# Layout changes by DVE blocks and DMA in place of TensorE transposes, in a two-layer mLSTM + RG-LRU trunk

## The chip, the cores and the metric

The kernel runs on one core of a Trainium2 chip. The metric is the device time of one execution in microseconds; where several runs are given, their median. A profile is one more execution, recorded instruction by instruction. Engines: PE (TensorE: matmuls; PEld its weight loads), DVE (VectorE), ACT (ScalarE), POOL (GpSimd), SP (SyncE, which here only issues DMAs).

## The reference

Two layers of one mixer, then a final RMSNorm; batch 1, 256 positions, width 2048, all in float32. Cut to what matters:

```python
def hybrid_layer(x, ...):
    u = rms_norm(x, norm_g)
    qk, v, o, z_a, ig, fg, xb, z_b = split(u @ w_in)            # w_in 2048 x 12304
    q, k = split(silu(causal_dwconv(qk, qk_conv)))              # 8 heads, width 128; v: width 256
    h = mlstm_chunkwise(q, k * DK ** -0.5, v, ig + i_bias, log_sigmoid(fg + f_bias))
    h = layernorm_per_head(h * sigmoid(o)) * head_norm_g
    y_a = h * silu(z_a)
    xc = causal_dwconv(xb, lru_conv_w) + lru_conv_b
    y_b = rg_lru(xc, w_a, b_a, w_x, b_x, lam) * silu(z_b)       # h_t = a_t h_(t-1) + u_t
    return x + concatenate([y_a, y_b]) @ w_out                  # w_out 4096 x 2048
for l in range(2): x = hybrid_layer(x, ...)
return rms_norm(x, final_g)
```

## The kernel before

Weights pass once from DRAM through SBUF. Every float32 product is made of three matmuls with split operands: H (high part, rounded to the fast float32 form) times H, H times L (the rest), L times H. For activations the split parts are `x_s` (the layer's input, channels on partitions), `yaH`/`yaL` and `ybH`/`ybL` (outputs of the two branches); for weights `wH` (cast on ACT, L289) and `wL` (subtraction on DVE, L160).

The work of a layer is cut into four groups `g` of 512 columns (two heads, 512 recurrent channels). A group has the chunks `o`, `qk`, `v`, `xb`, `z`, `zb` (each x times 2048 x 512 of `w_in`), a `gate` unit (the recurrent gates' matrices) and, for the group before, four `out` chunks. A chunk is four units of 1 MB of weights; a unit is two halves, and a half is 12 matmuls of 128 x 128 by 512 columns. `_sequence` lists the units in the order in which PE takes them. The last loop of `tile_trunk` goes over the halves: it prepares the split of the half three further on (`AHEAD`), records the half's matmuls, calls its `after` function (evacuation of the accumulator) and then `pump`, which lets the generators in `bg` (conv, attention, gates, norms) record some of their steps up to a budget. `None` or `"wait"` from a generator ends its turn. `require(key)` runs generators until a result is recorded. The split buffers are four deep (`wsp`), the raw weights three units (`wraw`). Each engine then runs its instructions in the order in which they stand; only data decide when.

Accumulators of the usual form hold tokens on partitions. Where channels are wanted on partitions there are three ways. PE transposes 128 x 128 blocks with an identity (L651 `ps_ty` for `ya`, 8 for each layer and group, in `z_post`; L851 `ps_tx` for the next layer's input, 8 for each of 4 chunks, in `out_chunk`). `to_channels` (for `qk`, `xb` and `zb`) writes a permuted copy `tok`, transposes 32 x 32 blocks on DVE (L404, `blk`), writes the rows to DRAM by four DMAs of SP (L407, `moved`) and reads them back by one of POOL (L408, `fr`). And a chunk named by `_by_channel` (only `zb` of layer 0, group 3) is multiplied with the operands exchanged (`mm_b`, L321), so that channels come out on partitions at once.

At the layers' border the four last `out` chunks add to `x_acc`; each is squared and summed for the norm, stored, transposed and split into the next layer's `x_s` (`split_xT`, L807 and L163). Layer 1 starts with its chunk `o`; the gates' scan (`gates_gen`, tiles `scs`) and the small transposition of `sT` (L495) hang on the end of that chunk.

## Time and profile before

| | us |
|---|---|
| median of 3 runs | 1513.75 (1512.88 to 1514.87) |
| the profiled execution | 1514.09 |
| its span in the trace | 1512.4 |
| PE busy | 1494.3 (99%) |
| DVE busy | 1040.6 (69%) |
| ACT busy | 907.0 (60%) |

A page's groups give, for one line, engine, operation and tile: count, busy time, mean duration in ns, and the idle time of the engine just before with what ended it. A timeline row gives start, duration, engine, line, operation, tiles written and read, form and count; in brackets the idle time of the engine before it and its releaser. A windows row gives from:to, length, the busy time and count of PE, PEld, DVE, ACT and POOL, PE's granted clock, the DMA engines' busy share and GB/s. A row of the waits: who waited for whom, total, times, longest.

### The profile page before, as it was taken

How to read it: one execution, taken by the hardware profiler on the slowest of the kernel's cores; microseconds unless marked ns; L12 is line 12 of the kernel's file. 1: busy time of each engine (PE TensorE's matmuls, PEld its weight loads, DVE VectorE, ACT ScalarE, POOL GpSimd, SP SyncE). 2: the span in 40 equal slices, each digit the busy share in tenths (PEclk: the TensorE clock that was granted, in tenths of full speed). 3: DMA queues.
4: the chain of work that ended last, by engine and by line, in shares of the span. 5: the costliest groups of instructions: out<-in, count | busy, mean ns of one | idle time of the engine just before them, and what ended most of it. 6: DMA issues, size and time to landing. Idle time of an engine off the chain costs nothing.

```text
span 1512.4 us, 18554 instructions
## 1 busy us (share of the span) xinstructions
PE 1494.3 (99%) x6980; PEld 1248.3 (83%) x6980; DVE 1040.6 (69%) x1406; ACT 907.0 (60%) x1142; POOL 66.4 (4%) x127
## 2 busy tenths in 40 slices
PE   8999999999999999999999999999999999999997
PEld 6888888888888888888888888888888888888886
DVE  6778666876567754778657786567855678556775
ACT  6658545675456754558654685466755567555674
POOL 0001000100000000000000000001000000000002
PEclk9999999999999999999999999999999999999999
DMA  9764658756577566885665656678566775577773
GB/s 329 286 212 168 217 214 250 233 191 223 192 254 225 193 223 213 256 255 195 213 205 191 229 177 221 209 232 245 181 221 218 230 231 198 200 229 268 233 244 108
DMA packets 82729, 333.07 MB, mean 220 GB/s; under 512 B 9024, under 2 KB 23376, under 8 KB 61136
## 3 DMA queue, kind: packets, MB, share of 16 engines
q1 hardware_dynamic: 72128, 299.40, 57.0%
q0 software_dynamic: 7760, 27.81, 8.1%
q10 hardware_dynamic: 2752, 4.69, 0.9%
q8 instruction: 54, 0.88, 0.2%
q14 instruction: 35, 0.29, 0.1%
HBM read 300.91 MB, written 30.95 MB: 219 GB/s over the span
## 4 chain that ended last, share of the span: by engine, by line
PE 91%; DMA 4%; DVE 3%; ACT 1%; issue 1%; SPq 0%; ACTq 0%; DVEq 0%
PE acc L307 27%; PE acc L306 27%; PE acc L308 27%; DMA raw<-in_ws_dram 3%; PE ps_gt L699 3%; PE acc L321 1%; DVE wL L160 1%; DVE xc L163 1%; PE acc L927 0%; ACT wH L289 0%; PE acc L928 0%; PE acc L929 0%; PE ps_ty L651 0%; DMA nb<-nG_d 0%; DMA nG_d<-scs 0%
## 5 line engine op out<-in xcount | busy, mean ns | idle before, releaser
L160 DVE TENSOR_TENSOR wL<-raw,wH 128x1024 fp32r<-128x1024 f32 (+1 forms) x526 | 638.1, 1216 | 362.9 <-ACT wH L289 362.3
L289 ACT CAST wH<-raw 128x1024 fp32r<-128x1024 f32 (+1 forms) x526 | 549.0, 1047 | 426.2 <-PE acc L308 394.0
L306 PE MATMUL acc<-wH,x_s 128*128 128x512 f32 x1504 | 587.9, 391 | 6.3 <-ACT wH L289 6.3
L307 PE MATMUL acc<-wL,x_s 128*128 128x512 f32 x1504 | 587.4, 391 | 2.0 <-DVE wL L160 2.0
L308 PE MATMUL acc<-wH,x_s 128*128 128x512 f32 x1504 | 586.4, 390 | 0.0
L306 PEld LDWEIGHTS acc<-wH,x_s 128*128 128x128 f32 x1504 | 283.0, 188 | 64.8 <-ACT wH L289 6.5
L307 PEld LDWEIGHTS acc<-wL,x_s 128*128 128x128 f32 x1504 | 283.0, 188 | 62.7 <-DVE wL L160 4.9
L308 PEld LDWEIGHTS acc<-wH,x_s 128*128 128x128 f32 x1504 | 283.0, 188 | 58.6
L306 PE MATMUL acc<-wH,yaH 128*128 128x512 f32 x224 | 87.9, 392 | 0.0
L306 PE MATMUL acc<-wH,ybH 128*128 128x512 f32 x224 | 87.4, 390 | 0.0
L308 PE MATMUL acc<-wH,yaL 128*128 128x512 f32 x224 | 87.3, 390 | 0.0
L308 PE MATMUL acc<-wH,ybL 128*128 128x512 f32 x224 | 87.3, 390 | 0.0
L307 PE MATMUL acc<-wL,ybH 128*128 128x512 f32 x224 | 87.3, 390 | 0.0
L307 PE MATMUL acc<-wL,yaH 128*128 128x512 f32 x224 | 87.2, 389 | 0.0
L401 ACT ACTIVATE tok<-acc,rstd 128x512 f32<-128x512 f32 x46 | 29.1, 685 | 38.2 <-PE acc L308 38.2
L308 PEld LDWEIGHTS acc<-wH,yaL 128*128 128x128 f32 x224 | 42.0, 188 | 9.0
L308 PEld LDWEIGHTS acc<-wH,ybL 128*128 128x128 f32 x224 | 42.0, 188 | 8.9
L307 PEld LDWEIGHTS acc<-wL,ybH 128*128 128x128 f32 x224 | 42.1, 188 | 8.3
L306 PEld LDWEIGHTS acc<-wH,ybH 128*128 128x128 f32 x224 | 42.1, 188 | 8.3
L307 PEld LDWEIGHTS acc<-wL,yaH 128*128 128x128 f32 x224 | 42.1, 188 | 8.1
L306 PEld LDWEIGHTS acc<-wH,yaH 128*128 128x128 f32 x224 | 42.1, 188 | 8.1
L832 ACT COPY stage<-acc 128x1024 f32<-128x1024 f32 x24 | 24.4, 1015 | 38.9 <-PE acc L308 38.9
(209 smaller groups left out, 1332.8 us busy)
## 6 DMA issues: line engine op xcount, KB each, us to landing
raw<-in_ws_dram SPq DMA_DIRECT2D x168, 1024.0 KB, 4.9
raw<-in_ws_dram SPq DMA_DIRECT2D x190, 512.0 KB, 4.8
x_d<-stage POOLq DMA_DIRECT2D x24, 512.0 KB, 6.8
moved<-blk SPq DMA_DIRECT2D x92, 128.0 KB, 2.3
fr<-moved POOLq DMA_DIRECT2D x23, 512.0 KB, 4.8
x_d<-x_acc ACTq DMA_DIRECT2D x8, 512.0 KB, 8.0
x_acc<-x_d SPq DMA_DIRECT2D x8, 512.0 KB, 5.0
xp<-in_xt_dram SPq DMA_DIRECT2D x8, 256.0 KB, 7.9
```

Of the source, the lines that this page charges most:

```text
L160: return V.tensor_tensor(out=o, in0=a, in1=b, op=op)
L163: return V.scalar_tensor_tensor(out=o, in0=a, scalar=s, in1=b, op0=op0, op1=op1)
L289: S.copy(out=H[:, o], in_=r[:, o])
L306: PE.matmul(o, a_H[:, kt, tsl], Hv[:, k], start=s, stop=False)
L307: PE.matmul(o, a_H[:, kt, tsl], Lv[:, k], start=False, stop=False)
L308: PE.matmul(o, a_L[:, kt, tsl], Hv[:, k], start=False, stop=e)
L321: PE.matmul(ps[:, ct, T * part : 2 * T], W[:, k, P * ct : P * ct + P], moving, start=first and k == 0 and part == 0, stop=last and k == 3 ...
L401: S.activation(out=tok[:, :, :, t, :].rearrange("p m c j -> p c m j"), in_=acc[:, t, :].rearrange("p (c m j) -> p c m j", c=4, m=4), func= ...
L699: PE.matmul(o, W[:, ib, jl], xs[:, ib, a, :], start=j == 0 and i == 0 and W is Hv and a == 0, stop=i == 1 and W is Lv, skip_group_check=True)
L832: S.copy(out=stage, in_=ps)
```

## The change

Six things change.

1. PE transposes no more 128 x 128 blocks. `ya` goes the way of `to_channels`: `z_post` writes `tok` by DVE, `swapped` does the 32 x 32 transposition and the DMAs, `split_channels` makes `yaH` and `yaL` out of `fr`, after `LANDING` (4) turns. The next layer's input goes the same way in `out_chunk`, with a second pair of `tok`/`blk` in the buffer `qs` for the odd chunks.
2. The border's splits are no generator: they are recorded a fixed number of halves (`BORDER`, 7) after their chunk.
3. The first two chunks of layer 1, `o` and `qk`, go by turns unit by unit; each unit's quarter of the contraction needs one quarter of `x_s`. The last four `out` chunks: the first two still by turns, the others one after the other.
4. `zb` of group 0 comes before `z` of the same group (it came in group 1); group 1 has `qk`, `o`, `v`.
5. `zb` of group 3 goes by channel in layer 1 too.
6. `require` and `drain` go round the generators where one says "wait"; the transposition of `sT` waits two (layer 0) or four (layer 1) turns more; `zb` waits for `hz`, the product of head output and gate, instead of `yT`.

```diff
@@ _sequence
-            head = {0: ("o", "qk", "v"), 1: ("o", "zb", "v", "qk")}.get(g, ("o", "v", "qk"))
-            items = [("in", l, k, 0 if k == "zb" else g) for k in head]
+            head = {0: ("o", "qk", "v"), 1: ("qk", "o", "v")}.get(g, ("o", "v", "qk"))
+            items = [("in", l, k, g) for k in head]
             items += fill[0:2] + [("in", l, "xb", g)] + fill[2:4]
-            items += [("in", l, "z", g), ("gate", l, g)] + ([("in", l, "zb", g)] if g > 0 else [])
-            seq += [u for it in items for u in units(it)]
+            items += [("in", l, "z", g), ("gate", l, g)]
+            items.insert(len(items) if g > 0 else -2, ("in", l, "zb", g))
+            us = [u for it in items for u in units(it)]
+            if l > 0 and g == 0:
+                us[0:8] = [us[i] for i in (0, 4, 1, 5, 2, 6, 3, 7)]
+            seq += us
         if l + 1 < DEPTH:
-            for c in (0, 2):
-                u = units(("out", l, NG - 1, c)) + units(("out", l, NG - 1, c + 1))
-                seq += [u[i] for i in (0, 2, 1, 3)]
+            u = [u for c in range(4) for u in units(("out", l, NG - 1, c))]
+            seq += [u[i] for i in (0, 2, 1, 3, 4, 5, 6, 7)]
@@ _by_channel
-    return (l, kind, g) == (0, "zb", NG - 1)
+    return (kind, g) == ("zb", NG - 1)
@@ to_channels, split
+    def swapped(tok, blk=None):
...
+    def split_channels(fr, scale, H, L):
+
+        ch = new_tok().rearrange("p m c t j -> p m (c t j)")
+        for ct in range(4):
+            S.activation(out=ch[:, ct].rearrange("p (t a i) -> p t a i", t=2, a=4),
+                         in_=fr[:, :, ct].rearrange("p a t i -> p t a i"), func=AF.Copy, scale=scale[:, ct : ct + 1])
+        S.copy(out=H, in_=ch)
+        tt_(L, ch, H.bitcast(F32), ALU.subtract)
@@ gates_tr
+        for _ in range(2 + 2 * l):
+            yield "wait"
@@ z_post
-            tt_(hf, hf, za, ALU.mult)
...
-                        PE.transpose(out=pt[:, 256 * c + P * t : 256 * c + P * t + P],
-                                     in_=hf[:, t, P * ct : P * ct + P], identity=ident)
...
+            tok = new_tok()
+            for t in range(2):
+                tt_(by_block(tok, t), hh[:, t].rearrange("p h (c m j) -> p (h c) m j", c=2, m=4),
+                    za[:, t, :].rearrange("p (c m j) -> p c m j", c=4, m=4), ALU.mult)
+            st["hz", l, g] = True
+            fr = swapped(tok)
+            yield 2.6
+            for _ in range(LANDING):
+                yield "wait"
+            split_channels(fr, pars[:, l, O_HG + 4 * g : O_HG + 4 * g + 4], yH, yL)
@@ out_chunk
+            for t in range(2):
+                tt_(by_block(tok, t), x_acc[:, t, cs].rearrange("p (c m j) -> p c m j", c=4, m=4),
+                    ps[:, t, :].rearrange("p (c m j) -> p c m j", c=4, m=4), ALU.add)
             xs = x_acc[:, :, cs]
             tt_(xs, xs, ps, ALU.add)
...
+            fr = swapped(tok, blk)
+            square_sum(c)
+            store_x(c)
+
+            def split():
+                xn = st["x_n"][:, 4 * c : 4 * c + 4]
+                split_channels(fr, pars[:, l + 1, O_NG + 4 * c : O_NG + 4 * c + 4], xn[:, :, 0, :], xn[:, :, 1, :])
+                st["xT", l + 1, c] = True
+            timed.append((st["n"] + BORDER, split))
@@ the loop over halves
+        while timed and timed[0][0] <= n:
+            timed.pop(0)[1]()
```

Three places show how instructions move. **First place**, DVE, layer 1, group 0, at the product of `z` with its sigmoid (`za`); `dn`, `hh`, `bs`, `mv` are the head outputs and their statistics, `xc` conv steps. Before:

```order
L163 SCALAR_TENSOR_TENSOR hh<-ps_n,dn,so 128x256 x2
L611 BN_STATS bs<-hh 128x6 x2
L612 BN_AGGR mv<-bs 128x2
L163 SCALAR_TENSOR_TENSOR dn<-ps_n,em 128x1
L612 BN_AGGR mv<-bs 128x2
L163 SCALAR_TENSOR_TENSOR za<-acc,rstd,sz 128x512
L160 TENSOR_TENSOR dn<-dn,ps_n 128x1
L163 SCALAR_TENSOR_TENSOR xc<-ch,pars,xc 128x253
L608 RECIPROCAL dn<-dn 128x1
L160 TENSOR_TENSOR wL<-raw,wH 128x1024
```

and in the change:

```order
L167 SCALAR_TENSOR_TENSOR hh<-ps_n,dn,so 128x256
L645 BN_STATS bs<-hh 128x6
L646 BN_AGGR mv<-bs 128x2
L164 TENSOR_TENSOR wL<-raw,wH 128x1024
L650 RECIPROCAL sd<-sd 128x4
L172 TENSOR_SCALAR hh<-hh,mv,sd 128x256 x4
L164 TENSOR_TENSOR wL<-raw,wH 128x1024 x3
L167 SCALAR_TENSOR_TENSOR za<-acc,rstd,sz 128x512
```

The conv steps and the head statistics are over when `za` comes, and three weights' low parts stand directly ahead of it.

**Second place**, ACT, the same group, after the gate unit (`gate_...` are the two gates, `Dt` the decay). Before:

```order
L679 CAST xcs<-xc 128x2x256
L615 ACT_TABLE_LOAD
L615 ACTIVATE sd<-mv,epst 128x4
L704 ACT_TABLE_LOAD
L704 ACTIVATE gate_7207<-ps_gt,pars 128x256 x4
L704 ACTIVATE gate_7243<-ps_gt,pars 128x256 x2
L289 CAST wH<-raw 128x1024
L704 ACTIVATE gate_7243<-ps_gt,pars 128x256 x2
L289 CAST wH<-raw 128x1024 x3
```

and in the change:

```order
L300 CAST wH<-raw 128x1024
L729 ACTIVATE gate_7413<-ps_gt,pars 128x256 x4
L741 ACT_TABLE_LOAD
L741 ACTIVATE Dt<-gate_7378,sp_103 128x256 x4
L747 ACTIVATE gate_7378<-gate_7378,sp_102 128x256 x4
L300 CAST wH<-raw 128x1024 x2
```

The decay's eight activations follow the gates without a cast between; the casts that stood among them come after.

**Third place**, ACT at the layers' border, `junk` being the squares for the norm. Before, for one chunk:

```order
L380 ACTIVATE junk,ss<-x_acc 128x512
L117 DMA x_d_81<-x_acc 256x1x512
L380 ACTIVATE junk,ss<-x_acc 128x512
L807 ACTIVATE x_s<-ps_tx,pars 128x256 x2
L289 CAST wH<-raw 128x1024
L807 ACTIVATE x_s<-ps_tx,pars 128x256 x2
```

and in the change, where chunk 0's copy is first read:

```order
L391 ACTIVATE junk,ss<-x_acc 128x512
L121 DMA x_d_83<-x_acc 256x1x512
L391 ACTIVATE junk,ss<-x_acc 128x512
L442 ACTIVATE tok<-fr,pars 128x256 x4
L300 CAST wH<-raw 128x1024
L444 CAST x_s<-tok 128x4x256
```

The split of chunk 0 now stands behind the squares of chunk 2 (`x_d_83`), two chunks later than its own.

More of the change, by code (lines that the diff above doesn't have):

```diff
@@ L29 @@
 LANDING = 4
+BORDER = 7
 def _nunits(item):
@@ L209, in tile_trunk @@
     bg = deque()
+    timed = []
     def pump(budget):
@@ L227, in require, with step @@
     def require(key):
+        i = 0
         while key not in st:
-            try:
-                next(bg[0])
-            except StopIteration:
-                bg.popleft()
+            i = step(i)
+    def step(i):
+        i %= len(bg)
+        try:
+            return i + 1 if next(bg[i]) == "wait" else 0
+        except StopIteration:
+            del bg[i]
+            return 0
     def drain():
+        i = 0
         while bg:
-            for _ in bg.popleft():
-                pass
+            i = step(i)
     halves = []
@@ L347, in chunk_in @@
                             u == 0 and i == 0, u == 3 and i == 1, paired) for i in range(2)]
-                add_unit(mms, before=beforefn if u == 0 else None,
+                add_unit(mms, before=(lambda u=u: beforefn(u)) if beforefn else None,
                          after=(lambda: postfn(acc())) if u == 3 else None, paired=paired)
@@ L390, in conv, with new_tok, by_block @@
             stt(o[:, ct, d:T], x_[:, ct, 0 : T - d], wv[:, 3 - d : 4 - d], o[:, ct, d:T], ALU.mult, ALU.add)
+    def new_tok():
+        return work.tile([P, 4, 4, 2, 32], F32, tag="tok", name="tok")
+    def by_block(tok, t):
+        return tok[:, :, :, t, :].rearrange("p m c j -> p c m j")
     def to_channels(l, acc):
@@ L396, in to_channels @@
         rstd = st["rstd", l]
-        tok = work.tile([P, 4, 4, 2, 32], F32, tag="tok", name="tok")
-        blk = work.tile([P, 4, 256], F32, tag="blk", name="blk")
+        tok = new_tok()
+        for t in range(2):
+            S.activation(out=by_block(tok, t), in_=acc[:, t, :].rearrange("p (c m j) -> p c m j", c=4, m=4),
+                         func=AF.Copy, scale=rstd[:, t : t + 1])
+        return swapped(tok)
+    def swapped(tok, blk=None):
+        if blk is None:
+            blk = work.tile([P, 4, 256], F32, tag="blk", name="blk")
         fr = work.tile([P, 4, 4, 2, 32], F32, tag="fr", name="fr", bufs=2)
-        for t in range(2):
-            S.activation(out=tok[:, :, :, t, :].rearrange("p m c j -> p c m j"),
-                         in_=acc[:, t, :].rearrange("p (c m j) -> p c m j", c=4, m=4), func=AF.Copy,
-                         scale=rstd[:, t : t + 1])
         V.transpose(out=blk.rearrange("p m n -> p (m n)"), in_=tok.rearrange("p m c t j -> p (m c t j)"))
@@ L509, in e_gen @@
         yield None
+        while ("aT", l) not in st:
+            yield "wait"
         E = small.tile([P, 2, 384], F32, tag="E", name="E", bufs=1)
@@ L639, in gen @@
             hh = st["hn", l, g]
[L640 to L659 removed]
+            tok = new_tok()
+            for t in range(2):
[5 more added lines that the diff above has]
+            for _ in range(LANDING):
+                yield "wait"
+            split_channels(fr, pars[:, l, O_HG + 4 * g : O_HG + 4 * g + 4], yH, yL)
+            yield 1.2
             st["yT", l, g] = True
@@ L754, in gen @@
                 yield "wait"
-            while ("lru", l, g) not in st or ("yT", l, g) not in st and g > 0:
+            while ("lru", l, g) not in st or ("hz", l, g) not in st:
                 yield "wait"
@@ L838, in postfn @@
             x_acc = st["xa"]
+            if c % 2:
+                two = work.tile([P, 2, 1024], F32, tag="qs", name="tokblk")
+                tok = two[:, 0].rearrange("p (m c t j) -> p m c t j", m=4, c=4, t=2)
+                blk = two[:, 1].rearrange("p (m n) -> p m n", m=4)
+            else:
+                tok, blk = new_tok(), None
+            for t in range(2):
+                tt_(by_block(tok, t), x_acc[:, t, cs].rearrange("p (c m j) -> p c m j", c=4, m=4),
+                    ps[:, t, :].rearrange("p (c m j) -> p c m j", c=4, m=4), ALU.add)
             xs = x_acc[:, :, cs]
             tt_(xs, xs, ps, ALU.add)
-            st["credit"] -= 1.1
-            def gen():
-                square_sum(c)
-                store_x(c)
-                yield None
-                for b in range(2):
-                    pt = aux("ps_tx")
-                    for j in range(2):
-                        for t in range(2):
-                            PE.transpose(out=pt[:, 256 * j + P * t : 256 * j + P * t + P],
-                                         in_=x_acc[:, t, 512 * c + 256 * b + P * j : 512 * c + 256 * b + P * j + P],
-                                         identity=ident)
-                    split_xT(l + 1, c, pt.rearrange("p (j t) -> p j t", j=2), (4 * c + 2 * b, 4 * c + 2 * b + 1))
-                    yield 0.8
-            bg.append(gen())
+            fr = swapped(tok, blk)
[6 more added lines that the diff above has]
+            timed.append((st["n"] + BORDER, split))
         for half_src in range(2):
@@ L865, in layer_start, with before @@
     def layer_start(l):
-        def first_before():
-            drain()
+        def before(u):
             if l > 0:
                 st["x"] = st["x_n"]
-        return first_before
+                assert ("xT", l, u) in st
+        return before
     def emit_in(l, kind, g):
@@ L1034, in tile_trunk @@
     for n, hf in enumerate(order_):
+        st["n"] = n
         while nprep < len(order_) and nprep <= n + AHEAD:
```

19 lines of the change are left out of this document (1 added, 18 removed).

## The prediction

> **What bounds the kernel now.** First the page: which engine is full, and who is in the chain of waits.
>
> ```profile
> PE 1494.3 (99%) x6980; PEld 1248.3 (83%) x6980; DVE 1040.6 (69%) x1406; ACT 907.0 (60%) x1142; POOL 66.4 (4%) x127
> ...
> PE 91%; DMA 4%; DVE 3%; ACT 1%; issue 1%; SPq 0%; ACTq 0%; DVEq 0%
> ...
> L651 PE MATMUL ps_ty<-ident,hh 128*128 128x128 f32 x64 | 8.3, 272 | 0.0
> L851 PE MATMUL ps_tx<-ident,x_acc 128*128 128x128 f32 x32 | 4.1, 272 | 0.0
> ```
>
> PE is busy 99% of the span and makes 91% of the chain. "Busy" flatters it, because the ends of pipelined matmuls are modelled; the honest measure is the distance from one start to the next. In a steady stretch of the timeline that is:
>
> ```profile
> 640.00 0.39 PE L308 MATMUL acc<-wH,yaL 128*128 128x512 f32 x1
> ...
> 647.48 0.39 PE L308 MATMUL acc<-wH,ybL 128*128 128x512 f32 x1
> ```
>
> 33 steps of one matmul of 512 columns lie between these rows: 0.227 us each. A half unit (12 such matmuls) is 2.72 us, a unit 5.44 us. The program is a row of such halves, and PE time taken out of it shortens the span one for one, as long as the weights' splits on ACT and DVE keep pace. The places where they do not are the idle times before PE in the timeline:
>
> ```profile
> 72.17 0.39 PE L308 MATMUL acc<-wH,x_s 128*128 128x512 f32 x1
> 73.16 0.31 PE L495 MATMUL ps_sT<-ident,scs 64*128 64x64 f32 x2 [0.60 <-DVE scs L163]
> ...
> 142.91 1.03 PE L651 MATMUL ps_ty<-ident,hh 128*128 128x128 f32 x8
> 143.70 0.48 PE L306 MATMUL acc<-wH,x_s 128*128 128x512 f32 x1
> 144.59 0.50 PE L307 MATMUL acc<-wL,x_s 128*128 128x512 f32 x1 [0.41 <-DVE wL L160]
> ...
> 879.02 0.39 PE L306 MATMUL acc<-wH,x_s 128*128 128x512 f32 x1
> 880.97 0.50 PE L307 MATMUL acc<-wL,x_s 128*128 128x512 f32 x1 [1.56 <-DVE wL L160]
> ...
> 1480.81 0.39 PE L929 MATMUL acc_x<-wH,yaL 128*128 128x512 f32 x1
> 1482.17 0.50 PE L927 MATMUL acc<-w_own,ybH 128*128 128x512 f32 x1 [0.97 <-ACT ybH L769]
> ```
>
> Two lie in the first group of a layer (143.70 in layer 0, 879.02 in layer 1), where PE waits for a weight's low part on DVE; one waits for the gates' scan (73.16); one, near the end, for the second branch's output.
>
> **The change part by part.** Removed from PE: 96 transposes (64 of L651, 32 of L851), always 8 in a row. Eight of them take 143.70 - 142.91 = 0.79 us on PE's clock of starts, so 12 rows of eight cost 9.5 us. That is a gain at once, PE being the bound. **-9.5.**
>
> Added to PE: the last group's gate chunk of layer 1 goes by channel (L321's form), as layer 0's does today:
>
> ```profile
> 688.21 1.32 PE L321 MATMUL acc<-x_s,wH 128*128 128x512 f32 x5
> ...
> 711.43 0.40 PE L306 MATMUL acc<-wH,yaH 128*128 128x512 f32 x1
> ```
>
> 711.43 - 688.21 less 0.79 for the eight transposes that stand within it is 22.4 us for that chunk; in the usual form it is 96 steps of 0.227 = 21.8. **+0.7** (rounded up). In return the output of that chunk no longer goes out to DRAM and back. Today PE waits for it, 1482.17 - 1480.81 - 0.23 = 1.1 us. The way that it takes now:
>
> ```profile
> 1459.48 1.27 ACT L401 ACTIVATE tok<-acc,rstd 128x512 f32<-128x512 f32 x2 [1.67 <-PE acc L308]
> ...
> 1460.78 1.25 DVE L404 STREAM_TRANSPOSE blk<-tok 128x1024 f32<-128x1024 f32 x1 [0.36 <-ACT tok L401]
> ...
> 1475.21 1.06 ACT L762 ACTIVATE zsg<-fr 128x1024 f32<-128x1024 f32 x1 [0.59 <-DMA fr<-moved]
> ```
>
> By channel, the 15.7 us up to 1475.21 fall away; what is left are some eight steps like this one of layer 0,
>
> ```profile
> L160 DVE TENSOR_TENSOR zb<-zb,acc 128x512 f32<-128x512 f32 x2 | 1.4, 678 | 0.0
> ```
>
> 5.4 us, against 8 halves of products with the other branch (22 us) that PE does first. **-1.1**; zero at worst, if another late weight takes its place.
>
> The first group of each layer. Its gate chunk is put ahead of `z` and the gates, so that conv work, head statistics and `z` no longer meet. In the first place where the order is shown above, the `wL` (the low part of a half's weights) that PE awaited stood behind a long run of small work; now three stand in a row there. The run's length is in DVE's timeline:
>
> ```profile
> 872.49 1.21 DVE L160 TENSOR_TENSOR wL<-raw,wH 128x1024 fp32r<-128x1024 f32 x1
> ...
> 879.71 1.21 DVE L160 TENSOR_TENSOR wL<-raw,wH 128x1024 fp32r<-128x1024 f32 x1
> ```
>
> 7.2 us between two low parts, where a half has 2.72. With it go 880.97 - 879.02 - 0.23 = 1.7 us and, in layer 0, 144.59 - 143.70 - 0.23 = 0.7 us. **-2.4.** What comes late next is ACT, after the gates: the second place shows twelve activations and a table load between two of its casts. Its rows, with the table load and the cast itself:
>
> ```profile
> L704 ACT ACTIVATE gate<-ps_gt,pars 128x256 f32<-128x256 f32 x64 | 26.2, 486 | 2.9 <-PE ps_gt L699 2.9
> L716 ACT ACTIVATE Dt<-gate,sp 128x256 f32<-128x256 f32 x32 | 15.3, 506 | 0.1
> L722 ACT ACTIVATE gate<-gate,sp 128x256 f32<-128x256 f32 x32 | 14.4, 502 | 0.0
> L716 ACT ACT_TABLE_LOAD x8 | 10.3, 1283 | 0.1
> L289 ACT CAST wH<-raw 128x1024 fp32r<-128x1024 f32 (+1 forms) x526 | 549.0, 1047 | 426.2 <-PE acc L308 394.0
> L160 DVE TENSOR_TENSOR wL<-raw,wH 128x1024 fp32r<-128x1024 f32 (+1 forms) x526 | 638.1, 1216 | 362.9 <-ACT wH L289 362.3
> ACT wH L289 <- PE acc L308: 394.0, 291, 2.2
> ```
>
> 4 x 0.486 + 1.283 + 4 x 0.506 + 4 x 0.502 = 7.3 us. The last row says what a cast normally waits for: the buffer that PE gives back (four of them). So a cast may start three halves, 8.2 us, ahead of its use; after the cast (1.05) and the low part (1.2) 5.9 us of slack are left. The 7.3 us of work replace 2.72 - 1.05 = 1.7 us that ACT has between two casts anyhow, so they put the next cast 5.6 us back: just inside, if ACT comes into them on time. Bounds: 0, and what this stage loses today, 0.7 and 1.7. I take 0.4 in each layer, nearer to zero because of that 0.3 of room: **+0.8.**
>
> The gates' scan. In layer 0 the small transposition of `sT` (L495) is put two halves later, past the wait: 73.16 - 72.17 - 0.23 = 0.76, **-0.7.** In layer 1 it also moves, but so does the scan, which starts six halves later because chunk `o` is done by turns with `qk`. It then shares DVE with eight conv steps that stood behind it before:
>
> ```profile
> L163 DVE SCALAR_TENSOR_TENSOR qc<-ch,pars,qc 128x255 f32<-128x255 f32 (+2 forms) x96 | 41.3, 481 | 4.0 <-ACT qc L386 3.6
> ```
>
> 8 x 0.48 = 3.8 us. The transposition of `sT` now stands nine halves behind the gates' products instead of eight, which gives 2.7 us back. Bounds 0 and 3.8; I take **+0.4**, near to the lower, since DVE had idle time there too.
>
> The layers' border. The new input's split reads a copy that went through DVE's 32x32 transposition, four writes to DRAM (SP) and one read (POOL). In the third place shown above, the reader of chunk 0's copy stands behind chunk 2's squares: six casts, so six halves or 16.3 us, after the transposition's own place on DVE. What the trip takes:
>
> ```profile
> L407 SPq DMA_DIRECT2D moved<-blk x92: 325/432/1028, 60.9 to 1463.4; - x92
> DMA to landing us min/median/max: 2.0/2.4/8.2
> DMA to landing us min/median/max: 3.6/4.8/8.2
>   DMA fr<-moved: 2.3, 3
> ACT wH L289 <- DMA raw<-in_ws_dram: 13.2, 10, 2.1
> ```
>
> (The first four are from the views of the tiles `moved`, SP's part, and `fr`, POOL's; the issues are min, median and max in ns.) Transposition 1.25, three issues ahead of the last 1.3, landing 2.4 and landing 4.8: 9.8 us at the medians and POOL's own issue, 14.4 in the instance of 1460.78. Both fit into 16.3, and today's 23 trips ended only three waits, 2.3 us together. The same six halves stand between the two at the eight copies of `ya`; at the end of each layer PE then still has the gates and the gate chunk's 22.4 us between `z` and the use. Behind SP's waits for `blk` stand weight loads; they have three buffers, 16 us, and ACT loses 13.2 us over the whole run to late ones. So the trips cost **0**, with bounds below under the rivals. ACT and DVE pay a little more per copy than they did for the split out of PSUM:
>
> ```profile
> L657 ACT ACTIVATE yaH<-ps_ty,pars 128x256 fp32r<-128x256 f32 x32 | 13.3, 466 | 0.3 <-PE ps_ty L651 0.3
> L163 DVE SCALAR_TENSOR_TENSOR yaL<-ps_ty,pars,yaH 128x256 fp32r<-128x256 f32 x32 | 13.9, 476 | 0.2 <-ACT yaH L657 0.2
> ```
>
> ACT had 4 x 0.47 = 1.9 and has four such and a cast, 2.9; DVE had 4 x 0.48 = 1.9 and has a transposition and a low part, 2.5. Their idle shares of 40% and 31% hide it; in a stage where DVE is full it would be 0.6 us of PE per copy.
>
> The Trainium skill, page "VectorE: DVE Perf Modes", section "Rules for kernel authors", says to use TensorE for a 128x128 transposition where PSUM will do as the destination, which is against this change. By its table of three paths (390 ns on TensorE, in another type) 96 of them would be an estimated 37 us and the sum would begin with that; the trace has 9.5, and that is used. The rule weighs a single transposition, and does not ask which engine is full.
>
> **The sum.** -9.5 + 0.7 - 1.1 - 2.4 + 0.8 - 0.7 + 0.4 = -11.8 us, against the profiled execution's 1514.09: 1502.3. That execution lies 0.3 above the median of the runs, 1513.75, so 1502.0 is the forecast.
>
> **The rivals.** (a) Everything hidden is a gain: no stall arises (+1.2 falls away), and the waits removed had smaller companions too short for the idle column, some 1 us in all. 1499.8, at least 1497.5. For it: the new order spreads work everywhere. Against: seven places get a new wait.
>
> (b) The border is late. There four copies (4 x 1.05 MB written and read) and the stores come on top of weights:
>
> ```profile
> 740.00:780.00 40.00, 40.00 (x189) 33.36 (x188) 25.62 (x36) 25.34 (x41) 1.52 (x2) 1.00 0.66 225
> 20.00:40.00 20.00, 20.00 (x95) 16.69 (x94) 11.84 (x19) 13.67 (x28) 0.00 (x0) 1.00 1.02 382
> ```
>
> 4.2 MB over some 49 us is 86 GB/s more than 225, against 382 that the start moves. It fits, but transfers come in bursts. If each quarter is 1 to 2 us late, 4 to 6 us go: 1507.
>
> (c) Slower: the in-order queue of ACT. A copy that lands late holds up the reader on ACT, behind it every weight cast, and PE idles at each of the twelve new copies. A trip starts to cost above 16.3 + 3.9 = 20.2 us (3.9 is the casts' slack of 5.9 less four scaled copies of 0.5). With both landings at their longest (8.2 each) and a wait of 2 us in a queue it takes 21.6; at twelve copies 1.4 us each are 16.8, more than the gain: 1518.8. It decides from 1.0 us per copy. Against it: the three short waits in 23 trips.
>
> The skill's rule of above stands on this side: what a plain transposition on PE costs is known, what its way round costs is not.
>
> (d) No change: PE's time is not what bounds; the weights are, and the freed time comes back as waits. Then it stays at 1513.75. Against it: a steady 0.227 us step over hundreds of microseconds, and casts that wait for PE, not for DMA.
>
> **How the numbers follow.** Forecast 0.63 (1499.5 to 1504.5); (a) 0.10; (b) 0.18; (c) 0.06; (d) 0.03. The range, 1497.5 to 1507, takes in (a) and half of (b). About 0.2% is what a measurement here can tell from no change: 3 us, so forecast, (a) and (b) are all faster, 0.91; (d) is the 0.03 for the same, (c) the 0.06 for slower.
>
> **What would show it.** Right: no `ps_ty` and `ps_tx` on PE, start-to-start steps of 0.227 through both borders, no idle column at the gates of either first group, no wait for `ybH` near the end. Wrong: idle before PE with "DMA fr<-moved" or "ACT x_s" at 720 to 790, ACT waiting for `fr` by more than a few us in all, or a longer wait at `ps_sT` in layer 1 (the +0.4).

## The result, and the profile after

The changed kernel takes 1498.99 us (median of four runs, 1498.60 to 1499.61); the kernel before, run beside it, 1513.68. The ratio is 0.9903, with a 95% interval of 0.9886 to 0.992: 14.7 us faster, 3 us under the forecast of 1502.0. The profiled execution is the one of 1498.6 us.

The page of the kernel after, its engines and its chain of waits:

```profile
PE 1481.1 (99%) x6916; PEld 1239.3 (83%) x6916; DVE 1053.3 (70%) x1403; ACT 916.0 (61%) x1153; POOL 79.2 (5%) x138
...
PE 97%; DVE 1%; DMA 0%; ACT 0%; issue 0%; SPq 0%; DVEq 0%; ACTq 0%
```

PE's share of the chain goes from 91% to 97%: nearly nothing but PE's own row is left. PE's waits after (who waited for whom: us in all, times, longest):

```profile
PE acc L317 <- ACT wH L300: 6.6, 1, 6.6
PE acc L317 <- DVE x_acc L164: 0.8, 1, 0.8
PE acc L318 <- DVE wL L164: 0.4, 1, 0.4
```

The first is the start of the program, which the kernel before has too (6.3). The waits for `wL` in the first groups, for the scan and for `ybH` are gone. The second is new.

**A measure for single parts.** The times of one kernel's runs lie up to 4 us apart, and the first 30 us alone, where the first weights land, differ by up to 1.4 us from trace to trace. So beside the medians I use D, the time in one trace from PE's 97th matmul (the first of tile `ps_g`, at 31 us, the same place in every kernel here) to its last. Of the kernel before, then of the kernel after, the two rows of PE's timeline are:

```profile
31.76 0.28 PE L449 MATMUL ps_g<-x_s,gwp 128*104 128x256 f32 x1
...
1504.14 0.28 PE L929 MATMUL acc<-wH,ybL 128*128 128x256 f32 x1
```

```profile
31.19 0.28 PE L479 MATMUL ps_g<-x_s,gwp 128*104 128x256 f32 x1
...
1488.66 0.28 PE L956 MATMUL acc<-wH,ybL 128*128 128x256 f32 x1
```

D is 1472.38 before and 1457.47 after, 14.9 less. What follows the last matmul is 8.2 us in both. A second trace of the kernel before gives 1472.15. That is the only repeat, so D is taken as good to 0.2 or 0.3, and a difference of that size is at its limit.

**The new wait** stands at the layers' border, in the timelines of DVE and (last row) PE after:

```profile
750.34 1.28 DVE L164 TENSOR_TENSOR tokblk<-x_acc,acc 128x512 f32<-128x512 f32 x2
751.54 1.22 DVE L164 TENSOR_TENSOR wL<-raw,wH 128x1024 fp32r<-128x1024 f32 x1
752.67 1.22 DVE L164 TENSOR_TENSOR x_s<-tok,x_s 128x1024 fp32r<-128x1024 f32 x1
753.81 1.22 DVE L164 TENSOR_TENSOR x_acc<-x_acc,acc 128x1024 f32<-128x1024 f32 x1
...
755.17 0.47 PE L317 MATMUL acc<-wH,x_s 128*128 128x512 f32 x1 [0.80 <-DVE x_acc L164]
```

The accumulator is read by two sums into `tok` and by one into `x_acc`, and the last of them stands behind a weight's low part and a split. PE gets the buffer back at 755.03. Its step before is 1.19 us where 0.23 is usual.

**The copies through DRAM.** Who waited for `fr` after (us, times):

```profile
  ACT ch L449: 11.0, 4
  DVE zb L164: 4.6, 4
  ACT tok L442: 1.5, 1
```

L442 reads the twelve new copies. Only one of them kept ACT waiting, the border's last, for 1.5 us. The eight of `ya` landed 2.2 to 5.7 us before ACT came to them. The 11.0 us at L449 are waits for copies of `qk` and `xb`, which the kernel before makes too. There ACT waits 1.7 us for them, and 2.3 us for all copies. Of the longer waits now, one of 4.2 us at 118 us is there with the new order of groups alone (3.6 in the run `before_zb_early` below), and two of 3.4 and 3.1 us, at 194 and 934, are missing with `ya` back on PE. So ACT's waits for copies rise from 2.3 to 12.5 us. The prediction had named that as a sign of being wrong, but PE has no wait at any of these places.

### The profile page after: what moved, and what is told of

Its sections match the earlier page's. It is cut to its first block, busy times and chain, and to the rows that moved or that the text cites. A ratio compares the mean times of both kernels' runs of the same rounds, so it can differ in the third digit from the quotient of the medians.

```text
span 1496.9 us, 18541 instructions
## 1 busy us (share of the span) xinstructions
PE 1481.1 (99%) x6916; PEld 1239.3 (83%) x6916; DVE 1053.3 (70%) x1403; ACT 916.0 (61%) x1153; POOL 79.2 (5%) x138
## 4 chain that ended last, share of the span: by engine, by line
PE 97%; DVE 1%; DMA 0%; ACT 0%; issue 0%; SPq 0%; DVEq 0%; ACTq 0%
PE acc L317 29%; PE acc L318 29%; PE acc L319 29%; PE ps_gt L724 3%; PE acc L332 3%; PE acc L955 1%; PE acc L954 1%; PE acc L956 1%; DMA raw<-in_ws_dram 0%; PE acc_x L954 0%; PE acc_x L955 0%; PE acc_x L956 0%; DVE wL L164 0%; PE ps_n L562 0%; PE ps_n L560 0%; PE ps_n L561 0%
## 5 line engine op out<-in xcount | busy, mean ns | idle before, releaser
L317 PE MATMUL acc<-wH,x_s 128*128 128x512 f32 x1472 | 574.3, 390 | 7.4 <-ACT wH L300 6.6
L318 PE MATMUL acc<-wL,x_s 128*128 128x512 f32 x1472 | 574.0, 390 | 0.4 <-DVE wL L164 0.4
L319 PE MATMUL acc<-wH,x_s 128*128 128x512 f32 x1472 | 573.2, 389 | 0.0
L317 PEld LDWEIGHTS acc<-wH,x_s 128*128 128x128 f32 x1472 | 276.7, 188 | 65.1 <-ACT wH L300 6.6
L318 PEld LDWEIGHTS acc<-wL,x_s 128*128 128x128 f32 x1472 | 276.7, 188 | 58.6 <-DVE wL L164 1.9
L319 PEld LDWEIGHTS acc<-wH,x_s 128*128 128x128 f32 x1472 | 276.7, 188 | 57.6
L429 POOL DMA_DIRECT2D fr<-moved x34 | 18.9, 555 | 724.2 <-DMA moved<-blk 426.7
L425 DVE STREAM_TRANSPOSE blk<-tok 128x1024 f32<-128x1024 f32 x32 | 39.7, 1240 | 12.7 <-ACT tok L415 12.6
```

Of the source, the lines that this page charges most:

```text
L317: PE.matmul(o, a_H[:, kt, tsl], Hv[:, k], start=s, stop=False)
L318: PE.matmul(o, a_H[:, kt, tsl], Lv[:, k], start=False, stop=False)
L319: PE.matmul(o, a_L[:, kt, tsl], Hv[:, k], start=False, stop=e)
L425: V.transpose(out=blk.rearrange("p m n -> p (m n)"), in_=tok.rearrange("p m c t j -> p (m c t j)"))
L429: G.dma_start(out=fr.rearrange("p a c t i -> p a (c t i)"), in_=moved)
```

## The experiments

### Each part undone, or done alone

First the transposes. `ya` back on PE:

```diff
-            fr = swapped(tok)
...
-            split_channels(fr, pars[:, l, O_HG + 4 * g : O_HG + 4 * g + 4], yH, yL)
+                        PE.transpose(out=pt[:, 256 * c + P * t : 256 * c + P * t + P],
+                                     in_=hf[:, t, P * ct : P * ct + P], identity=ident)
```

> The changed kernel with one part undone: the 64 transposes of ya (8 for each layer and group) stand on PE again, and nothing else is undone. Theory (PE's row of instructions sets the end, and what is taken out of it counts its start-to-start time, no more and no less): 8 rows of eight at 0.79 us come back, +6.3 us against the changed kernel's 1499.0, so 1505.3; the idle times before PE stay as they are in the changed kernel. Rival 1 (a transposition costs PE more than its own 0.79 us, because the matmuls round it lose their pace or the evacuation out of PSUM holds an accumulator: the 3 us beyond the forecast came from there): 96 transposes would be worth 12.5 us, 64 of them 8.3, so 1507.3. Rival 2 (the copies through DRAM cost PE hidden waits of their own, which go away with them): 1503 or less.

Measured: 1505.87 us (1504.78 to 1506.48), ratio to the kernel before 0.9943 (0.9931 to 0.9956); D 1464.32, 6.85 more than the changed kernel.

```profile
L686 PE MATMUL ps_ty<-ident,hh 128*128 128x128 f32 x64 | 8.3, 272 | 0.0
```

The theory holds: 6.9 by the medians, 6.85 by D, against 6.3. Rival 2 is out, and of rival 1 the size is out. A row of eight costs 0.86 us by D, 0.07 more than the 0.79 between its own starts, so a little of rival 1 is there. The steps show where it stands. The first matmul behind a row has 0.31 us to the next one, where 0.227 is usual. In PE's timeline of the kernel before, behind the row at 325.15:

```profile
325.94 0.48 PE L306 MATMUL acc<-wH,x_s 128*128 128x512 f32 x1
326.25 0.40 PE L307 MATMUL acc<-wL,x_s 128*128 128x512 f32 x1
```

Why that step is longer isn't shown.

The border's transposes back on PE, by a generator as before, with the change's order of units:

```diff
-            fr = swapped(tok, blk)
-            square_sum(c)
-            store_x(c)
...
+                        PE.transpose(out=pt[:, 256 * j + P * t : 256 * j + P * t + P],
+                                     in_=x_acc[:, t, 512 * c + 256 * b + P * j : 512 * c + 256 * b + P * j + P],
+                                     identity=ident)
```

> The changed kernel with one part undone: at the layers' border the 32 transposes of the next layer's input stand on PE again, split out of PSUM, by a generator as before; the order of the units stays that of the change. Theory: 4 rows of eight at 0.79 us come back, +3.2, and the one new wait of the changed kernel, 1.1 us at 754 us (PE waits for an accumulator that DVE's sum into x_acc still reads, behind two sums into tok), goes away with the sums into tok: +2.1 in all, 1501.1. Rival 1 (a transposition costs more than its 0.79 us): +4.2 less 1.1, 1502.1. Rival 2 (that wait has to do with the border's order of units, not with the sums into tok): it stays, 1502.2, and the idle time before PE at 754 is there again.

Measured: 1501.28 us (1500.95 to 1502.02), ratio 0.9915 (0.9902 to 0.9929); D 1459.94, 2.47 more. Its transposes and the only wait of PE that its trace has:

```profile
L876 PE MATMUL ps_tx<-ident,x_acc 128*128 128x128 f32 x32 | 4.1, 272 | 0.0
...
PE acc L317 <- ACT wH L300: 6.8, 1, 6.8
```

So the wait at 754 came with the way through `tok` and DRAM, and not with the order of units. That it was the sums, the run with the sum into `x_acc` first shows below. Without that wait of 1.0 us, the 32 transposes are worth 2.47 + 1.0 = 3.5 us.

Then the order of the groups. `zb` of group 0 back in group 1:

```diff
-            head = {0: ("o", "qk", "v"), 1: ("qk", "o", "v")}.get(g, ("o", "v", "qk"))
-            items = [("in", l, k, g) for k in head]
+            head = {0: ("o", "qk", "v"), 1: ("o", "zb", "v", "qk")}.get(g, ("o", "v", "qk"))
+            items = [("in", l, k, 0 if k == "zb" else g) for k in head]
```

> The changed kernel with one part undone: zb of group 0 stands in group 1 again (behind that group's o, with v and qk after it), in both layers. Theory (the stalls of the first groups come from DVE's long run where conv, head statistics and z meet, and the change of order took them away): idle before PE comes back where za of group 0 is made, 1.1 us in layer 0 and 2.5 in layer 1 by the sums over start-to-start steps before the change (the forecast had 0.7 and 1.7, the two idle columns alone): +3.6, 1502.6. Rival (the stalls went away because the transposes of ya left PE, DVE and ACT at that place): the order is worth nothing now, 1499.0 within 0.5.

Measured: 1504.09 us (1502.65 to 1504.65), ratio 0.9932 (0.9919 to 0.9946); D 1461.83, 4.36 more. Of PE's waits and timeline:

```profile
PE acc L318 <- DVE wL L164: 3.5, 3, 2.4
...
141.25 0.39 PE L317 MATMUL acc<-wH,x_s 128*128 128x512 f32 x1
144.00 0.50 PE L318 MATMUL acc<-wL,x_s 128*128 128x512 f32 x1 [2.36 <-DVE wL L164]
```

A stall is back, without one transpose of `ya` on PE, so the order matters by itself. It isn't the old stall again: layer 0 now loses most (2.5 us at 141.25), where in the kernel before layer 1 did. And it has another make. In DVE's timeline of this run DVE waits 2.45 us for `sd` on ACT, until 137.75, and the awaited low part (at 142.77) then stands behind the head outputs, the products into `tok` and the block transposition of `ya`, which the change brought. So this run alone doesn't size the order. The next one does.

The same edit the other way, alone, in the kernel before:

> The kernel before with one part of the change alone: zb of group 0 ahead of z and the gates of the same group, and qk, o, v in group 1; all 96 transposes stay on PE. Theory (as for the undoing of it): -3.6 us, 1510.1 against 1513.7, with no idle time before PE at the first groups (143 and 880 us). The forecast's term had -2.4 and +0.8 for ACT after the gates, -1.6: 1512.1. Rival (the stalls went away because the transposes of ya left): 1513.7 within 0.5.

Measured: 1509.30 us (1508.39 to 1509.63), ratio 0.9967 (0.9954 to 0.9979); D 1467.60, 4.7 less than the mean of the two traces before. PE's waits in full:

```profile
PE acc L307 <- ACT wH L290: 6.5, 1, 6.5
PE acc L308 <- DVE wL L161: 0.9, 2, 0.7
PE ps_sT L496 <- DVE scs L164: 0.6, 1, 0.6
```

So the order removes the stalls with all 96 transposes still on PE, and the rival is out. The 4.7 is more than the 3.6 that the theory had. The two stalls of the first groups are gone (0.7 of the 0.9 for `wL` stands in the first 20 us), no wait on ACT has come in their place, and one wait is missing that the theory did not count: `ybH`, near the end, though in this kernel that chunk still goes through DRAM. That put the term for the last group in doubt.

### The wait near the end

Layer 1's last `zb` back to the usual form:

```diff
-    return (kind, g) == ("zb", NG - 1)
+    return (l, kind, g) == (0, "zb", NG - 1)
```

> The changed kernel with one part undone: zb of group 3 goes by channel in layer 0 alone, as before; in layer 1 it goes out to DRAM and back again. Theory of the forecast (by channel took away the wait for ybH near the end, and costs a little of PE): the wait comes back (1.3 us by start-to-start steps) and 0.5 of PE time is saved (22.3 against 21.8 for the chunk), +0.8: 1499.8. Rival (the wait for ybH went for another reason: it is gone too in the kernel before with zb of group 0 put early, where this chunk still takes the way through DRAM): no wait near the end, and the 0.5 us saved show alone: 1498.5.

Measured: 1498.97 us (1498.82 to 1499.45), ratio 0.9905 (0.9891 to 0.9918); D 1457.17, 0.30 less. PE has no wait for `ybH` in this trace's list. One step there is 0.38 us where 0.23 is usual. The forecast's cause is refuted: going by channel in layer 1 did not remove the wait of 1.1 us, which is gone without it. By the steps in the changed kernel the chunk takes 22.34 us by channel, 0.6 more than 96 usual ones. By D it costs 0.3 net, at the limit of what D can tell, and it saves at most 0.2 or 0.3 at `ybH`.

Was the wait an accident of one execution? The kernel before, run and traced a second time:

> The kernel before as it is, for a second trace of it. In the first one the wait for ybH near the end (1.1 us net) hangs on ACT, where the cast of ybH at 1481.50 stands behind two casts that waited for a weight load to land (at 1479.60). Theory (that load was late in that one execution): the wait for ybH isn't in the second trace, while the waits for wL at 144 and 881 and for the scan at 73 are there again, with the same lengths within 0.2. Rival (it belongs to the program): the wait for ybH of about 1 us is there again. The idle times of the first 20 us (3.7 us before, 2.2 to 3.3 in the other traces) are expected to differ by up to a microsecond, since nothing of the change lies there.

Measured: 1513.16 us, one run. The wait is there again, as are those at `wL` and the scan, each within 0.1:

```profile
PE acc L307 <- DVE wL L160: 1.9, 2, 1.6
PE acc L927 <- ACT ybH L769: 1.0, 1, 1.0
PE ps_sT L495 <- DVE scs L163: 0.6, 1, 0.6
...
1474.28 1.06 ACT L762 ACTIVATE zsg<-fr 128x1024 f32<-128x1024 f32 x1 [0.67 <-DMA fr<-moved]
1475.25 1.99 ACT L289 CAST w_own<-raw 128x1024 fp32r<-128x1024 f32 x2
1478.66 2.00 ACT L289 CAST wH<-raw 128x1024 fp32r<-128x1024 f32 x2 [1.42 <-DMA raw<-in_ws_dram]
1480.56 1.14 ACT L769 CAST ybH<-zb 128x512 fp32r<-128x512 f32 x2
```

So the rival is right: the wait belongs to the program before. The rows show how it comes about. ACT waits for the copy `fr` (0.7 us), and so DVE's product `zb` is late. Then ACT waits for a weight load, and the cast of `ybH` stands behind both. In the kernel before with `zb` early the same rows are

```profile
1470.78 1.06 ACT L763 ACTIVATE zsg<-fr 128x1024 f32<-128x1024 f32 x1
...
1473.66 2.01 ACT L290 CAST wH<-raw 128x1024 fp32r<-128x1024 f32 x2
1476.53 1.14 ACT L770 CAST ybH<-zb 128x512 fp32r<-128x512 f32 x2 [0.86 <-DVE zb L161]
```

with no wait for a DMA. The difference is in how long the transfers take. They are issued at the same distances, but in the DMA views of that stretch four weight loads take 7.0 us (median) and `fr` 8.2 in the first trace of the kernel before, 6.9 and 8.2 in the second, 5.2 and 6.2 with `zb` early. Why the same transfers take 2 us longer in one program, and that in both of its traces, stays open.

### The scan and the order at the border

The transposition of `sT` at its old place:

```diff
-        for _ in range(2 + 2 * l):
-            yield "wait"
```

> The changed kernel with one part undone: the small transposition of sT no longer waits two turns (layer 0) and four turns (layer 1) more. By the order of instructions it then stands 9 matmuls (2.0 us) earlier in layer 0 and 6 (1.4 us) earlier in layer 1. Theory (the wait of layer 0 was real and the later place took it away; in layer 1 the scan is just over in time): layer 0's idle time of 0.8 to 1.2 us comes back at 72 us, and in layer 1 at 823 us 0 to 0.5: +1.2, 1500.2. Rival (layer 1 has much DVE work beside the scan since o and qk go by turns, so that without the later place the loss there is the larger one): +1 in layer 0 and 1 to 2.5 in layer 1, 1501.0 to 1502.5. Rival 2 (the wait only moves: PE waits later for what it no longer awaits there): 1499.0.

Measured: 1500.36 us (1498.90 to 1500.61), ratio 0.9911 (0.9898 to 0.9925); D 1458.16, 0.69 more.

```profile
71.86 0.31 PE L525 MATMUL ps_sT<-ident,scs 64*128 64x64 f32 x2 [0.59 <-DVE scs L167]
...
823.93 0.33 PE L525 MATMUL ps_sT<-ident,scs 64*128 64x64 f32 x2 [0.44 <-DVE scs L167]
```

Both waits come, 0.6 and 0.4, as the theory had it. By D the whole is 0.7 rather than 1.2. The median's 1.4 has a scatter of 1.7 around it, and I take D.

Layer 1 without turns. The splits are then recorded 5 halves after their chunk, not 7:

```diff
-BORDER = 7
+BORDER = 5
...
-            if l > 0 and g == 0:
-                us[0:8] = [us[i] for i in (0, 4, 1, 5, 2, 6, 3, 7)]
```

> The changed kernel with one part undone: layer 1 begins with chunk o in one piece and then qk (no turns), and the border's splits are recorded 5 halves after their chunk instead of 7, as this order needs. The last quarter of x_s is now wanted 7 halves (19.1 us) after the last out chunk ended, instead of 13 (35.4 us). Theory (the trip through DRAM costs nothing only because the turns give it room): in the changed kernel the last out chunk ends at 748.8 us, its block transposition at 756.2, its copy lands at 768.8 and the split is done 4.5 us later, at 773.3; without turns PE wants it at 748.8 + 1.1 + 19.1 = 769.0, so PE idles for some 4.3 us there with x_s named: 1503.3. Rival (the room is not needed, the splits come in time all the same, since the readers on ACT now stand earlier): 1499.0 within 0.7.

Measured: 1503.66 us (1502.90 to 1506.60), ratio 0.9940 (0.9927 to 0.9952): 4.7 more, where the theory had 4.3. D, from the profiled execution, is 7.7 more. From the profiled execution, the slowest of the five, PE's wait and then the windows view (length, busy time and count of PE, PEld, DVE, ACT, POOL, granted clock, DMA share, GB/s):

```profile
767.81 0.79 PE L315 MATMUL acc<-wH,x_s 128*128 128x512 f32 x1 [4.15 <-ACT x_s L442]
...
755.00:763.00 8.00, 7.98 (x35) 6.66 (x36) 5.45 (x9) 3.69 (x5) 0.00 (x0) 1.00 0.94 311
768.00:773.50 5.50, 5.49 (x13) 3.97 (x14) 1.20 (x2) 0.00 (x0) 0.00 (x0) 0.50 0.82 269
```

The wait is of the expected length but for the third quarter, not the last: its split stands on ACT behind a weight cast that waits for PE, so that it starts at 764.17 though its copy had landed at 757.04. So what PE awaited was not the trip through DRAM but the split's place in ACT's order, and that the length fits is luck. The theory also did not have the second row of the windows. After the wait PE runs at a granted clock of 0.50, one matmul every 0.427 us, for more than 5 us; 12 of them lose 2.4 us. Whether the other four executions, 1.2 to 3.7 us shorter, were spared that isn't shown: they have no trace.

### What a late copy costs

One more copy in DRAM at each of the twelve new trips:

```diff
+        if hop:
+            again = dram.tile([P, 4, 256], F32, tag="again", name="again", bufs=2)
+            G.dma_start(out=again, in_=moved)
+            moved = again
         G.dma_start(out=fr.rearrange("p a c t i -> p a (c t i)"), in_=moved)
```

> The changed kernel with the cost under dispute doubled: at each of the twelve new copies (eight of ya, four at the border) the 512 KB in DRAM are copied once more, DRAM to DRAM, by POOL's queue, before they are read back. An estimate from the landings of the profile (2.4 for a write, 4.8 to 5.8 for a read): some 6.5 us more per trip, which so becomes 14 to 21 us. By the order of instructions ACT's readers stand one cast (2.7 us) later than without, two in group 0. In the changed kernel the copies of ya land 2.2 to 5.7 us before their reader starts, those of the border 5.0, 3.0, 3.3 and 0.1. Theory (a late copy costs PE nothing until ACT has been held longer than the slack of its casts, 5.9 us): ACT waits 0 to 2 us at ya, up to 5 at the border's last, all within the slack: 1499.0 to 1500. Rival (c) of the forecast, in its plainest form (while ACT is held, PE soon is): the waits of ACT, some 16 us in all, come out at PE: 1515.

Measured: 1508.12 us (1507.15 to 1508.77), ratio 0.9964 (0.9951 to 0.9976): 9.1 us more, and by D the same 9.1. From the end of the block transposition to the landing, the trips of `ya` become 14.2 to 17.2 us, those of the border 17.4 to 24.6. At `ya` nothing is lost: ACT waits at four of the eight, at most 1.2 us, and PE steps on at 0.227. All but some 0.5 us goes at the border, between 748 and 772 us. Rows of ACT, DVE and PE there, the sum of ACT's waits for these copies, and two windows:

```profile
756.84 1.71 ACT L446 ACTIVATE tok<-fr,pars 128x256 f32<-128x256 f32 x4 [3.85 <-DMA fr<-again]
...
759.52 1.23 DVE L164 TENSOR_TENSOR wL<-raw,wH 128x1024 fp32r<-128x1024 f32 x1 [3.51 <-ACT wH L300]
760.66 1.22 DVE L164 TENSOR_TENSOR x_s<-tok,x_s 128x1024 fp32r<-128x1024 f32 x1
761.80 1.21 DVE L164 TENSOR_TENSOR x_acc<-x_acc,acc 128x1024 f32<-128x1024 f32 x1
...
763.15 0.47 PE L317 MATMUL acc<-wH,x_s 128*128 128x512 f32 x1 [3.65 <-DVE x_acc L164]
...
ACT tok L446 <- DMA fr<-again: 12.2, 7, 3.8
...
753.70:756.70 3.00, 3.00 (x9) 2.32 (x8) 2.31 (x3) 0.00 (x0) 0.00 (x0) 0.50 1.00 397
764.00:767.00 3.00, 3.00 (x9) 2.33 (x8) 2.26 (x8) 2.41 (x4) 0.00 (x0) 0.50 0.88 261
```

The theory is right for `ya` and wrong for the border. The plainest form of rival (c) is wrong for `ya`, where 3.1 us of ACT's waits cost PE nothing. At the border, 3.85 us on ACT become 3.65 us on PE, by the way that rival (c) named and one step more: copy late, ACT held, the weight's cast behind it, DVE's low part behind that, the sum into `x_acc` behind that, and PE without an accumulator. The slack of the casts, 5.9 us, did not help, because what PE lacked was not a weight. With two shorter waits (1.4 and 0.9 us above a usual step) and two stretches of about 8 matmuls at a clock of 0.5, 0.2 us more each, PE loses some 9 us here, of which the changed kernel loses 1.0 already.

Three more copies:

```diff
+            for n in range(2):
+                again = dram.tile([P, 4, 256], F32, tag=f"again{n}", name="again", bufs=2)
+                G.dma_start(out=again, in_=moved)
+                moved = again
```

> As the run with one more copy in DRAM, with three more: some 19.5 us more per trip, 27 to 34 us in all, readers three or four casts (8 to 11 us) later at ya and one to four at the border. Theory: ACT is now held 19.5 - 8.2 - 3.2 = 8 us at each ya, 2.2 over the slack of 5.9, and 11 to 14 us at three of the border's copies, 5 to 8 over it; 18 + 20 us at most, and as a late copy also moves what comes after it, half of that at least: 1518 to 1537, slower than the kernel before, with idle time before PE whose releaser is a weight (wH) on ACT. Rival (the copies' order is made to fit whatever the trip takes, and nothing of it reaches PE): 1499 to 1502.

Measured: 1578.67 us (1577.49 to 1579.17), ratio 1.0430 (1.0415 to 1.0444), D 77.6 more. Trips of 26 to 43 us. Waits of PE, and of ACT for the copies:

```profile
PE acc L317 <- ACT x_s L452: 15.3, 2, 12.9
PE acc L962 <- ACT yaH L452: 14.1, 1, 14.1
PE acc L317 <- ACT yaH L452: 12.2, 1, 12.2
PE acc L317 <- ACT wH L300: 12.2, 4, 6.6
PE acc L318 <- DVE wL L164: 9.0, 9, 2.0
...
ACT tok L450 <- DMA fr<-again: 68.3, 12, 10.3
```

Slower than before by 65 us: the sign of the theory, at more than twice its size. Three waits of 12 to 14 us that it did not have are PE wanting the operand itself, `ya` of group 3 in each layer and `x_s` at the border, and each is followed by half clock again.

### Better than both

The sum into `x_acc` first, and `tok` copied from it, so that DVE reads the accumulator once:

```diff
-            for t in range(2):
-                tt_(by_block(tok, t), x_acc[:, t, cs].rearrange("p (c m j) -> p c m j", c=4, m=4),
-                    ps[:, t, :].rearrange("p (c m j) -> p c m j", c=4, m=4), ALU.add)
             xs = x_acc[:, :, cs]
             tt_(xs, xs, ps, ALU.add)
+            for t in range(2):
+                V.tensor_copy(out=by_block(tok, t), in_=x_acc[:, t, cs].rearrange("p (c m j) -> p c m j", c=4, m=4))
```

> The changed kernel with the border's sums in another order: the sum into x_acc comes first, out of PSUM, and tok is then copied from x_acc (two copies from SBUF in place of two sums out of PSUM), so that PSUM is read once and the accumulator comes free 1.3 us sooner. Theory (PE's new wait of 1.06 us at 754 us is for that accumulator, held by three reads in a row on DVE with other work between them): the wait goes, 1498.0, the best so far. Rival 1 (DVE is full there, and the copies get to their place later instead: the trip of the last chunk is 1.2 us later and PE waits for x_s): 1499.0. Rival 2 (the wait is for DVE's queue as a whole, the sum stands where it stood): 1499.0, with the same idle time at 754.

Measured: 1497.69 us (1496.83 to 1498.05), ratio 0.9894 (0.9879 to 0.9909); D 1456.73, 0.74 less.

```profile
749.52 1.22 DVE L164 TENSOR_TENSOR x_acc<-x_acc,acc 128x1024 f32<-128x1024 f32 x1 [0.21 <-PE acc L319]
...
752.93 0.76 DVE L873 COPY tokblk<-x_acc 128x512 f32<-128x512 f32 x2
```

The sum is over at 750.7 instead of 755.0, and the wait is gone. 0.4 of the 1.1 us is lost again between 80 and 100 us in this trace, where nothing was changed.

With layer 1's chunk in the usual form as well:

> Two edits on the changed kernel together: the border's sum into x_acc first and tok copied from it, and zb of group 3 by channel in layer 0 alone. Theory (the first takes away the wait of 1.06 us at the border; the second saves the 0.5 us that the chunk by channel costs PE, and the wait for ybH near the end doesn't come back): 1499.0 - 1.1 - 0.5 = 1497.4. Rival (by channel in layer 1 has a use after all): 1498.5 or more, with a wait for ybH.

Measured: 1497.54 us (1496.86 to 1498.45), ratio 0.9896 (0.9881 to 0.9911); D 1456.40, 1.07 less than the changed kernel. Of the 0.5 us expected from the second edit 0.3 is left by D; a short wait for `ybH` is there:

```profile
PE acc L953 <- ACT ybH L794: 0.2, 1, 0.2
```

The second edit's 0.3 is again at the limit of D, and by the medians the two versions can't be told apart. Both lie some 1.4 us under the changed kernel, which was run at another time; D is what speaks for them.

## Why the prediction was right or wrong

The direction, the range and the cause (PE is the bound, and what leaves it counts one for one) were right. The forecast was 3 us short of the gain. The result lies 0.5 us outside the band of 1499.5 to 1504.5 that had 0.63, and rival (a), which had 0.10, came nearest: 1499.8 against 1499.0. Both its reasons held: the stalls of 1.2 us that the sum had did not arise, and the waits removed had smaller companions, of 1.1 us.

| step of the prediction | forecast | measured | by |
|---|---|---|---|
| 96 transposes | -9.5 | -10.3 | 6.85 + 3.5, undone |
| chunk by channel in layer 1 | +0.7 | +0.3 | undone; +0.6 by its own steps |
| wait for `ybH` | -1.1 | -1.2 | steps in both traces before; another cause |
| stalls of the first groups | -2.4 | -3.5 | `zb` early alone: -4.7, less 1.2 for `ybH` |
| ACT after the gates | +0.8 | 0 | the same run |
| scan, layers 0 and 1 | -0.7 + 0.4 | -0.7 | layer 0's step at 72 us, 0.76 long before; layer 1 has no such wait before or after |
| trips through DRAM | 0 | 0 | one more copy costs nothing at `ya` |
| the border's sums | not seen | +1.0 | in the trace; gone in three runs |
| sum | -11.8 | -14.4 | D: -14.8 |

No run undoes the new rounds of `require` and `drain`, the other condition on which `zb` waits, or the order of the last four `out` chunks by themselves; the 0.4 between the sum and D leaves them little.

**The first groups** are the step that failed most, 1.1 + 0.8 of the 3 us. The -2.4 was made of the two rows with an idle time in brackets, and the smaller steps after each long one were put into rival (a). And the +0.8 charged a wait on ACT at a place where ACT had time. "Just inside, if ACT comes into them on time" was the right reading, and 0.4 per layer for it a guess on the wrong side. In layer 1 of the changed kernel the later place of `sT` is worth 0.4 (its wait comes back without it), so the +0.4 for the scan did not arise either.

**The wait for `ybH`** had the right size and the wrong cause, so its size is luck. The step said: by channel, so no way through DRAM, so no wait. The wait hung on transfers that take 2 us longer in the kernel before, and the new order of groups 0 and 1 alone removed it. By channel in layer 1 costs 0.3 us net.

**The transposes** were read from their own starts; what the matmul behind them loses, 0.07 to 0.09 per row of eight, is not in those. The first trace shows it already, one row further on (326.25 - 325.94 above).

**The border.** That the trips are hidden was right, the reason half so. The room behind the transposition was put at six halves, 16.3 us, at the border and at `ya`. By the trace after, from its start to its reader, it is 13.8 to 14.7 us at `ya` and 14.0 to 18.6 at the border, and the trips fit because they take 8.9 to 11.6 and 12.9 to 15.6, all but the border's last, whose reader waits 1.5 us. The turns of `o` and `qk` give the splits their place on ACT (without them 4.7 us go, while the awaited copy lies ready for 7.1). The room was reckoned for ACT's casts alone, 16.3 + 3.9 us. With trips of 17 to 25 us PE lost 9.1 there, more than half of it for want of an accumulator. And the step's 2.5 us of DVE work per copy left out the border's two sums into `tok` (1.28 us), and it counted new work as hidden by DVE's idle share, without asking which buffer it holds meanwhile: three reads in a row kept PE's accumulator, +1.0.

**The rivals.** (b) did not come. A loss of its size, 4 to 9 us at the border, came in two runs, but quarters of `x_s` that wait for a late copy are only 2.3 us of it (the waits of 1.4 and 0.9 us with one more copy), and the half clock behind them 1.6. (c) did not come either: in the changed kernel ACT waits 4.2 us for a copy at 118 us, and PE has no idle time there. Its mechanism is real with trips twice or three times as long, and at 26 us or more it makes the kernel slower than before. The point from which it decides was put at 20.2 us, transposition included. Counted so, trips of up to 18.4 us cost nothing at `ya`, while at the border those of 18.6 to 25.8 cost 9.1. Its 21.6 us for a slow trip is also too long: 1.25 + 1.3 + 8.2 + 8.2 + 2 is 21.0, as landings are counted from the start of the issue. At 0.8 us a copy that gives some 9 us in place of 16.8, and 1511, which is not slower. (d) is out: the freed time did not come back as waits.

## What to carry to other kernels

When one engine is full, work moved off it counts whole if every way round it ends before its reader; look for that room in the reader's place on its in-order queue, and also ask which buffer each moved instruction holds while it waits its turn. Cost a stall over the whole stretch, start to start, not by the idle column alone. And test the reason of a gain by undoing each part: here one part cost a little, and its supposed gain came from another.

## What the runs showed of the hardware

After PE had waited 4.15 us, its granted clock was 0.50 for more than 5 us and the matmuls of 512 columns came every 0.427 us instead of 0.227. The same follows the waits of 3.65 and of 12 to 14 us. So a wait of 4 us can cost 2 us more than its length. The Trainium skill, page "TensorE: Matmul & The Clock Gate", section "Part 1: The HAM clock gate (the "warmup" mystery)", has this: the clock falls to half after an idle window of about 3.4 us and comes back after as long a busy one, with 426.7 ns for such a matmul. The 0.427 agrees. In the run with one more copy half clock also followed two waits of 1.4 and 0.9 us with two matmuls between them. In the run with three more copies it followed a single wait of 2.04 us (until 1004.97). With `zb` late it did not follow one of 2.36 us (until 144.00). So a wait of 3.4 us was not needed here, and the length of a shorter one does not decide by itself. What does, the runs here don't show.

On DVE, two copies of 128x512 from SBUF to SBUF take 0.76 us (L873 above), the two sums of that size out of PSUM that they replace 1.28.

The weight loads (median) and the copy's read near the end of the kernel before take 7 and 8 us in both its traces, and 5 and 6 with one chunk moved far ahead of them. So in these two traces the landing times belong to the program and not to the execution.
